# A new memory order for the tiles of a one-core decoder kernel (YOCO trunk, Trainium2)

## The chip, the core and the metric

The kernel runs on one core of a Trainium2 chip. The metric is the device time of one execution in microseconds (us). Three runs of the kernel before gave 1237.50, 1237.68 and 1237.83 us; the median is 1237.68 us.

Five engines take part. PE multiplies matrices (PEld is its loading of weights), DVE does elementwise work and scans, ACT does activations, copies and casts, POOL clears a few tiles and issues some transfers, SP issues most transfers. Each engine works through its own list of instructions in order and waits at an instruction until the semaphores that it names are there.

## The reference, cut to what matters

The input x is 512 tokens by 1024 features. Two layers follow, then a last RMSNorm.

```
x = x + s5_mixer(rms_norm(x))          # layer 0
x = x + conv_ffn(rms_norm(x))
kv = rms_norm(x) @ kv_w                # shared keys and values
x = x + stick_breaking_attention(rms_norm(x), w_q, k, v, w_o)   # layer 1
x = x + conv_ffn(rms_norm(x))
out = rms_norm(x)
```

The mixer projects x (u = h @ w_in), runs a diagonal complex state-space recurrence with 64 states for each group of 16 channels, takes y = C s + D u, then gelu, then a full GLU projection (y @ w_glu, 1024 to 2048). The FFN projects up to 2 x 2816 features, puts a causal convolution of width 3 on the gate half, and projects down to 1024. Attention has 16 heads of 64.

## The kernel before, in words

**Stages.** The work goes through five stages, one after the other: the S5 mixer (lines 241 to 806, the first 225 us), the first FFN, attention, the second FFN, and the final norm inside the last down-projection. x stays on the chip all the time, features on the 128 partitions, 8 tiles of 128 x 512.

**The products.** Nearly all products are float32r products of a split operand: a weight tile is cast into a high part (`split_hi`, L155, on ACT), the rest becomes the low part (`split_lo`, L160, on DVE), and an input is split the same way. `gemm` (L165) then issues three matmuls for each slice of 128 input features: high weight with high input, high weight with low input, low weight with high input. A 128 x 512 output over 8 slices is 24 matmuls. In the profile all of them have line 106. The names of PE's products are: `u` (input projection), `kk`, `v`, `y`, `yt`, `bt` (pieces of the mixer), `gl` (GLU projection), `fg` and `fu` (up-projection, gate and linear half), `fd` (down-projection), `kqb` (keys and queries), `v` (values), `z` (scores) and `ob` (attention output and the output projection).

**Tiles and pools.** A tile of the on-chip memory comes from a pool, by a tag. Each tag of a pool has a fixed number of buffers, and each new tile of the tag takes the next of them in turn; it must wait until the last reader of the tile that was there before is done. Pools lie one above the other in memory in the order in which they are entered. In the kernel before that is, from low to high: `const` (x, parameters), `wp` (raw weights 3 x 4096 bytes, and the high and low weights, 3 x 4096 each), `tp` (split inputs: tag `ta`, 10 tiles of 2048 bytes, and `tb`, 3 of 4096), `sm` (18 small tiles of 16 bytes, for each of which 32 are set aside, and three of 2048), and then the pool of the stage, opened by `Work(name, tag=buffers, ...)` (L60) and closed at its end. Bytes are bytes of each partition here and below. `T` (L83) takes a tile from `tp` or from the stage's pool.

Counted from the tile sizes, the mixer's, the FFN's and the attention's pools begin behind `sm`, so their tiles lie 18 x 32 + 3 x 2048 = 6720 bytes above the end of `tp`, and 6720 is 13 x 512 + 64. In the built program the tiles of `wp` and `tp` begin 160 bytes above a multiple of 512 and those of the stages' pools 224 bytes above one.

**The mixer's loop.** It works in 8 units n (128 channels each), under a hand-written order for PE, DVE and ACT. For unit n, PE issues `kk` and `v_(n + 1)` (L631, 16 products in 32 records, which multiply the two transposed tiles `bts` of unit n + 1 with u; the first 8 read the first `bts`, the other 8 the second), then `y_in(n)`. DVE meanwhile forms `states(n)`: the product `p` of v(n), then `wv`, two additions that combine it (L664 and L665), the scans `rv`, a second `p`, and `xv`, on which PE's `y_state(n)` waits. Beside it DVE works on unit n + 2: `k`, `bn` (from which PE makes the transposes `bt`, copied by ACT into `bts`), `k`, `cm`. Small portions of the projections are put between (`fill`). From 155 us on PE runs the rest of the GLU projection without a break.

**Buffers that the change touches.** In the mixer `bts` has tag `bt` with 2 buffers, `wv` tag `wv` with 1, and `rv`, `xv`, `y8`, `tq` one each. In the FFN the tags `g`, `s` and `u` have 2, 2 and 3 buffers and `a` 24 (the split activations that `fd` reads). In attention `o`, `kv` and `tw` have 2, 2 and 4, and `aw`, `os` and `kq` (split weights of attention, split outputs, split keys and queries) 9, 16 and 8. Attention's own pool `at` (constants, low keys `kl`, values `vv`) is entered behind the stage's pool and lies above it.

Of the kernel before, what the change touches and what calls it, by code (L numbers as in the profile page):

```python
# [7 lines left out]
F32 = mybir.dt.float32  # L8
# [9 lines left out]
P = 128  # L18
S = 512
# [4 lines left out]
EPS = 1e-6  # L24
AW = 22
TP = {"ta": 10}
PRE = (11, 12, 10, 5, 3)
F = ((4, 0, 3, 0), (1, 1, 1, 1), (2, 1, 1, 0), (3, 1, 1, 3), (3, 2, 1, 1), (1, 1, 1, 0), (1, 2, 2, 3), (0, 0, 3, 3))
HALVES = 4
# [18 lines left out]
def trunk(ctx: ExitStack, tc: tile.TileContext, A, out):  # L48
    nc = tc.nc
    V, SC, PE, GP = nc.vector, nc.scalar, nc.tensor, nc.gpsimd  # L50

    const = ctx.enter_context(tc.tile_pool(name="const", bufs=1))
    wp = ctx.enter_context(tc.tile_pool(name="wp", bufs=3))
    tp = ctx.enter_context(tc.tile_pool(name="tp", bufs=1))
    sm = ctx.enter_context(tc.tile_pool(name="sm", bufs=2))
    dr = ctx.enter_context(tc.tile_pool(name="dr", bufs=3, space=DRAM))

    cur = {}

    class Work:  # L60


        def __init__(self, name, **bufs):
            self.name, self.bufs = name, bufs

        def __enter__(self):
            self.pool = tc.tile_pool(name=self.name, bufs=1)
            cur["w"] = (self.pool.__enter__(), self.bufs)

        def __exit__(self, *a):  # L70
            self.pool.__exit__(*a)
# [4 lines left out]
    def banks_by_tag(**bufs):  # L76

        ids = sorted(range(8), key=lambda i: max([n for n, u in enumerate(used) if u == i], default=-1))
        cur["p"] = {}
        for tag, n in bufs.items():  # L80
            cur["p"][tag], ids = ids[:n], ids[n:]

    def T(name, dt=F32, tag=None):  # L83
        if tag in TP:
            return tp.tile([P, S], dt, tag=tag, name=name, bufs=TP[tag])
        pool, bufs = cur["w"]
        return pool.tile([P, S], dt, tag=tag, name=name, bufs=bufs[tag])

# [10 lines left out]
    def B(name, tag="b"):  # L99
        ids = cur["p"][tag]  # L100
        ids.append(ids.pop(0))
        used.append(ids[-1])
        return ps.tile([P, S], F32, tag=f"b{ids[-1]}", name=name, bufs=1)
# [29 lines left out]


    def load_raw(src, cols, name="w", dma=None):
        raw = wp.tile([P, 8 * P], F32, tag="raw", name=name + "r", bufs=3)[:, :cols * P]
        (dma or nc.sync).dma_start(out=raw, in_=src)
        return raw

# [55 lines left out]
    def rstd(b, stag="st"):  # L195
        v = sm.tile([P, 4], F32, name="sv")
        ts(v, b[:, 0:4], 1.0 / 1024.0, EPS, MUL, ADD)
        it = sm.tile([P, 4], I32, name="si")
        ts(it, v.bitcast(I32), 1, op0=ALU.logical_shift_right)
        f = sm.tile([P, 4], F32, name="sf")  # L200
        V.tensor_copy(out=f, in_=it)
        yi = sm.tile([P, 4], I32, name="sy")
        ts(yi, f, -1.0, 1597463007.0, MUL, ADD)
        r = sm.tile([P, 4], F32, name="sr0")
        V.tensor_copy(out=r, in_=yi.bitcast(F32))
        for n in range(3):
            q = sm.tile([P, 4], F32, name="sq2")
            tt(q, r, r, MUL)
            stt(q, q, -0.5, v, MUL, MUL)
            r2 = sm.tile([P, 4], F32, name=f"sr{n + 1}")  # L210
            stt(r2, q, 1.5, r, ADD, MUL)
            r = r2
        dg = N("dg", "sq", 1)
        dg3 = dg.rearrange("p (a c) -> p a c", c=P)
        tt(dg3, bc(ident, 1, [P, 4, P]), bc(r, 2, [P, 4, P]), MUL)
        b2 = B("rbp", stag)
        mm(b2, ones, dg, True, True)
        rb = N("rb", "rb", 1)
        SC.copy(out=rb, in_=b2)
        return rb, r  # L220
# [20 lines left out]
    def s5(st_next):  # L241
        banks_by_tag(st=1, u=2, g=2, kb=1, v=1, y=1)
        with tc.tile_pool(name="s5", bufs=1) as sp, ExitStack() as wctx:
# [19 lines left out]
            u8s, ys = [], []  # L263
# [23 lines left out]
            tags = ("u", "u", "g", "g")  # L287

            def w_load(n, q):
                raw = wp.tile([P, 8 * P], F32, tag="raw", name="wi", bufs=3)  # L290
                for c in ((slice(0, 256), slice(256, 1024)) if n == 0 else (slice(0, 1024),)):
                    q.dma_start(out=raw[:, c], in_=A["w_in"][n][:, c])
                wis.append(raw)
# [41 lines left out]

            def load(k):

                raw = wp.tile([P, 8 * P], F32, tag="raw", name="wvr", bufs=3)
                for i in range(0, HALVES, 2):
                    GP.dma_start(out=raw[:, i * 2 * P:(i + 2) * 2 * P].rearrange("p (h c) -> p h c", h=2),  # L340
                                 in_=A["w_glu"][i // 2, :, :, k * P:(k + 2) * P].rearrange("h p c -> p h c"))
                raws.append(raw)
# [9 lines left out]
            def fill(n):  # L352
                for _ in range(n):
                    next(pe)
# [13 lines left out]
            def evac(now=True):  # L368
                while len(u8s) < (len(bus) if now else evac.ready):
                    u_out(len(u8s))  # L370
                evac.ready = len(bus)

            evac.ready = 0

            fill(PRE[0])
            bst = B("stat", "st")
# [9 lines left out]
            def s32(dt=F32):  # L386
                i = len(small)
                if i % 16 == 0:
                    blocks.append(T("small", tag=("rv", "xv", "y8")[i // 16]))
                small.append(blocks[-1][:, 32 * (i % 16):32 * (i % 16) + 32])  # L390
                return small[i] if dt == F32 else small[i].bitcast(dt)
# [6 lines left out]
            zc, k, r, p = s32(), s32(), s32(), s32()  # L398

            def exp_acc(z):  # L400
                ts(zc, z, -87.0, 88.0, MAX, MIN)
                ts(k, zc, 1.4426950408889634, MAGIC, MUL, ADD)
                ts(k, k, -MAGIC, op0=ADD)
                stt(r, k, -0.693359375, zc, MUL, ADD)
                stt(r, k, 2.12194440054690583e-4, r, MUL, ADD)
                cs = [1.0 / 5040, 1.0 / 720, 1.0 / 120, 1.0 / 24, 1.0 / 6, 0.5, 1.0]
                ts(p, r, cs[0])
                for c in cs[1:]:
                    stt(p, p, c, r, ADD, MUL)
                e = s32(dt=I32)  # L410
                ts(e, k, 127.0, 8388608.0, ADD, MUL)
                o = s32()
                stt(o, p, 1.0, e.bitcast(F32), ADD, MUL)
                return o

            dt = exp_acc(ldt)
# [81 lines left out]
            for g2 in range(2):  # L498
                rows, cols = slice(64 * g2, 64 * g2 + 64), slice(g2, 32, 2)
# [5 lines left out]
            rb, _ = rstd(bst)  # L505
            fill(PRE[1])
            evac()
# [106 lines left out]
            def op_b(n):  # L614

                unit[n] = {}
                k3 = products(b3, pw3, n, 1)
                yield
                bn = wide("bn", 2, "bn")
                sums(bn, k3)  # L620
                unit[n]["b"] = halves(bn)

            def bt_(n, i):
                pb = B("bt", "kb")
                for q in range(4):
                    PE.transpose(v4(pb)[:, q], v4(unit[n]["b"][i])[:, q], ident)
                bt = T("bts", tag="bt")
                SC.copy(out=bt, in_=pb)
                unit[n].setdefault("bt", []).append(bt)
# [98 lines left out]
            def run(gen, n=99):  # L728
                for _ in range(n):
                    if next(gen, True) is True:  # L730
                        return
# [5 lines left out]
            kx_(0)  # L737
            fill(PRE[2])
            bt_(0, 0)
# [5 lines left out]
            run(op_b(1))  # L745
            fill(PRE[3])
            bt_(1, 0)
# [5 lines left out]
            turn_products(1)  # L753
            fill(PRE[4])
            evac()
            decays(0)
            with tc.manual_schedule(engines={E.PE, E.DVE, E.Activation}):
                for n in range(KT):
# [18 lines left out]
                    y8 = y_state(n)  # L777
# [31 lines left out]


    def ffn(layer, prev, st_next):
        with Work(f"ff{layer}", a=24, g=2, acc=2, s=2, u=3, y=8, half=10):
            banks_by_tag(b=7, st=1)
            rb, _ = prev.st.finish()
            ffn_body(layer, prev.xs, rb, st_next)
# [38 lines left out]


    def attention(prev, st_next):
        with Work("att", aw=9, tw=4, os=16, o=2, kq=8, kv=2):
            banks_by_tag(z=6, d0=1, d1=1)
            rb, rtok = prev.st.finish("d0")
            with tc.tile_pool(name="at", bufs=1) as ap:  # L860
                attention_body(ap, prev.xs, rb, rtok, st_next)

    def attention_body(ap, xs, rb, rtok, st_next):
# [16 lines left out]
        class Weight:  # L880
# [2 lines left out]

            def load(self):
                if callable(self.src):
                    self.raw = wp.tile([P, 8 * P], F32, tag="raw", name="awr", bufs=3)
                    self.src(self.raw)
                else:
                    self.raw = load_raw(self.src, self.cols, "aw")
# [127 lines left out]
        kq, vvs, vws = {}, {}, {}  # L1017
# [210 lines left out]
        cur = Head(0)  # L1228
# [7 lines left out]
        with tc.manual_schedule(engines={E.PE, E.DVE, E.Activation}):  # L1236
            pend, late = [4], []
            for i in range(16):
# [79 lines left out]
                cur = nxt  # L1318
# [93 lines left out]

    stages = A.get("stages", 4)
    nx = Next(NFFN0)
    with Work("s5t", ys=16, k=1, bn=1, bt=2, p=1, wv=1, rv=1, xv=1, y8=1, tq=1):
        s5(nx)
    if stages > 1:
        n2 = Next(None)
# [72 lines left out]
```

## Time and profile before

| what | value |
|---|---|
| median of 3 runs | 1237.68 us |
| the profiled execution | 1236.96 us |
| its span, first to last instruction | 1235.2 us |
| mean granted clock of PE | 0.997 |
| PE busy | 1207.6 us, 98% of the span, 6411 records |
| DVE busy | 809.6 us, 66% |
| ACT busy | 539.3 us, 44% |
| DMA | 118.5 MB, 96 GB/s over the span |

The profile is one execution, recorded by the hardware. The profiled execution takes 1.8 us more than its span and 0.7 us less than the median of the runs. A PE record's own duration covers the filling and draining of the array, so the time that a row of matmuls takes is read from start to start: the chain of waits prints it, as the start of a group of instructions, its time on the chain, and the count.

### The profile page before, as it was taken

The numbers are of one execution on the slowest core, as the hardware profiler recorded it, in microseconds if no ns is written. First come the engines' busy times: TensorE is split into PE (matmuls) and PEld (weight loads), VectorE is DVE, ScalarE is ACT, GpSimd is POOL, SyncE is SP. The second block draws the span as 40 slices with busy tenths as digits, with TensorE's granted clock in tenths as the row PEclk, the third lists the DMA queues.
The fourth block names the chain that finished last, engine by engine and source line by source line (L and its number), as shares of the span: only waits on it lengthen the run. The fifth ranks groups of instructions, "written<-read, shape, count | busy, mean of one in ns | idle before, by whom it ended". The sixth has DMA issues, their size and how long they took to land.

```text
span 1235.2 us, 16227 instructions
## 1 busy us (share of the span) xinstructions
PE 1207.6 (98%) x6411; PEld 982.8 (80%) x6411; DVE 809.6 (66%) x1284; ACT 539.3 (44%) x866; POOL 24.2 (2%) x65
## 2 busy tenths in 40 slices
PE   7989999999999999999999999999999999999995
PEld 3457788788888888888889898888888888888884
DVE  7999764665435635557878989878655346536554
ACT  5234453433223323334577878765433233323331
POOL 1011020000000000000000000000000000000000
PEclk9999999999999999999999999999999999999998
DMA  5565443233233233233211211123233232332322
GB/s 199 150 166 140 122 124 98 86 102 98 90 102 99 82 106 101 92 91 100 76 51 53 82 55 48 39 86 103 86 102 97 91 103 86 91 113 88 94 75 69
DMA packets 55068, 118.47 MB, mean 96 GB/s; under 512 B 12912, under 2 KB 28528, under 8 KB 54992
## 3 DMA queue, kind: packets, MB, share of 16 engines
q1 hardware_dynamic: 50880, 105.55, 27.9%
q0 software_dynamic: 3248, 11.54, 3.1%
q8 instruction: 50, 0.82, 0.3%
q10 hardware_dynamic: 864, 0.35, 0.1%
q14 instruction: 26, 0.21, 0.1%
HBM read 109.03 MB, written 8.39 MB: 95 GB/s over the span
## 4 chain that ended last, share of the span: by engine, by line
PE 89%; DVE 8%; ACT 1%; issue 1%; DMA 1%; SPq 0%; DVEq 0%; ACTq 0%
PE fd L106 20%; PE fu L106 19%; PE fg L106 19%; PE kqb L106 7%; PE gl L106 6%; PE z L106 5%; PE ob L106 5%; PE v L106 4%; DVE k L112 2%; DVE p L112 1%; PE u L106 1%; PE y L106 1%; DVE cm L112 1%; DVE u L112 1%; DVE rv L670 1%
## 5 line engine op out<-in xcount | busy, mean ns | idle before, releaser
L106 PE MATMUL fd<-ah,wdh 128*128 128x512 f32 (+1 forms) x359 | 140.5, 391 | 0.0
L106 PE MATMUL fd<-ah,wdl 128*128 128x512 f32 (+1 forms) x359 | 139.2, 388 | 0.0
L106 PE MATMUL fd<-al,wdh 128*128 128x512 f32 (+1 forms) x359 | 137.9, 384 | 0.0
L112 DVE TENSOR_TENSOR x<-x,fd 128x512 f32<-128x512 f32 (+1 forms) x49 | 33.1, 676 | 119.8 <-PE fd L106 119.8
L157 ACT CAST wuh<-wur 128x1024 fp32r<-128x1024 f32 x44 | 46.4, 1054 | 134.4 <-PE fg L106 118.0
L157 ACT CAST wdh<-wdr 128x896 fp32r<-128x896 f32 (+1 forms) x48 | 47.1, 982 | 128.0 <-PE fd L106 98.2
L112 DVE TENSOR_TENSOR g<-fg,rb 128x512 f32<-128x512 f32 x44 | 30.4, 691 | 96.3 <-PE fg L106 93.5
L106 PE MATMUL fu<-xh,wuh 128*128 128x512 f32 x220 | 86.0, 391 | 0.0
L106 PE MATMUL fg<-xh,wgl 128*128 128x512 f32 x220 | 85.8, 390 | 0.0
L106 PE MATMUL fg<-xh,wgh 128*128 128x512 f32 x220 | 85.7, 390 | 0.0
L106 PE MATMUL fg<-xl,wgh 128*128 128x512 f32 x220 | 85.6, 389 | 0.0
L106 PE MATMUL fu<-xh,wul 128*128 128x512 f32 x220 | 85.6, 389 | 0.0
L106 PE MATMUL fu<-xl,wuh 128*128 128x512 f32 x220 | 85.6, 389 | 0.0
L112 DVE TENSOR_TENSOR u<-fu,rb 128x512 f32<-128x512 f32 x44 | 30.4, 691 | 80.5 <-PE fu L106 80.5
L106 PE MATMUL fu<-xhl,wuh 128*128 128x512 f32 x264 | 81.8, 391 | 0.0
L106 PE MATMUL fg<-xhl,wgh 128*128 128x512 f32 x264 | 81.5, 389 | 0.0
L106 PEld LDWEIGHTS fd<-ah,wdl 128*128 128x128 f32 x359 | 67.4, 188 | 15.2
L106 PEld LDWEIGHTS fd<-al,wdh 128*128 128x128 f32 x359 | 67.4, 188 | 14.8 <-issue 0.2
L106 PEld LDWEIGHTS fd<-ah,wdh 128*128 128x128 f32 x359 | 67.5, 188 | 13.2 <-issue 0.2
L157 ACT CAST wgh<-wgr 128x1024 fp32r<-128x1024 f32 x44 | 46.3, 1053 | 71.0 <-PE fd L106 33.0
L106 PE MATMUL u<-xg,wi 128*128 128x512 f32 x128 | 63.5, 628 | 7.5 <-ACT xg L270 7.5
L109 DVE SCALAR_TENSOR_TENSOR acc<-g,cw,acc 128x511 f32<-128x511 f32 x88 | 65.8, 747 | 2.4 <-ACT acc L832 0.9
(247 smaller groups left out, 2799.1 us busy)
## 6 DMA issues: line engine op xcount, KB each, us to landing
wgr<-in_w_up SPq DMA_DIRECT2D x44, 512.0 KB, 3.5
wur<-in_w_up SPq DMA_DIRECT2D x44, 512.0 KB, 3.5
wdr<-in_w_dn SPq DMA_DIRECT2D x32, 448.0 KB, 3.3
wdr<-in_w_dn SPq DMA_DIRECT2D x16, 512.0 KB, 3.5
wvr<-in_w_glu POOLq DMA_DIRECT2D x12, 512.0 KB, 3.8
ks<-kx SPq DMA_DIRECT2D x32, 128.0 KB, 2.5
m<-ks SPq DMA_DIRECT2D x8, 512.0 KB, 4.1
awr<-in_w_k SPq DMA_DIRECT2D x8, 512.0 KB, 3.5
```

The lines of the kernel that those rows point to most:

```text
L106: PE.matmul(o, lhsT=lhsT, rhs=rhs, start=start, stop=stop, skip_group_check=True)
L109: (eng or V).scalar_tensor_tensor(out=o, in0=a, scalar=s, in1=b, op0=op0, op1=op1)
L112: (eng or V).tensor_tensor(out=o, in0=a, in1=b, op=op)
L157: SC.copy(out=hi, in_=raw)
L670: V.tensor_tensor_scan(out=rv[:, c], data0=decay[n], data1=wv[:, c], initial=0.0, op0=MUL, op1=ADD)
```

## The change: what it does

The pools are entered in a new order, low to high: `const`, then `sm`, then a new pool `wr` for the raw weights, then a new pool `lw`, and only then `wp` (now the high and low weights alone), `tp`, and the stages' pools. In attention the pool `at` is entered ahead of the stage's pool, so that constants, low keys and values lie below the other tiles.

The pool `lw` holds tiles that PE mostly doesn't read. It has three tags of 2048-byte tiles: `la` with 2 buffers, `lb` with 2, `lc` with 4. Each `Work` now names which of its tags take their tiles there. In the FFN `g`, `s`, `u` become `la`, `lb`, `lc` (so `u` has 4 buffers where it had 3). In attention `o`, `kv`, `tw` become `la`, `lb`, `lc`, with the counts that they had. In the mixer `rv` becomes `la`; `wv` and `bt` together become `lb`; `tq`, `xv` and `y8` together become `lc`. So the two `bts` of a unit and `wv`, which had three buffers, now take two in turn, and `tq`, `xv`, `y8`, which had three, take four.

No instruction is added or taken away. In the built program the places change as follows (bytes of each partition):

| tiles | before | after |
|---|---|---|
| raw weights | from 34976 | from 41696 |
| high and low weights | 47264 to 71840 | 70368 to 94944 |
| split inputs `xh`, `xl` | 71840 to 92320 | 94944 to 115424 |
| split inputs `xhl` | 92320 to 104608 | 115424 to 127712 |
| GLU inputs `ys` | from 111328 | from 127712 |
| split activations `ah`, `al` | 129760 to 178912 | 131808 to 180960 |
| attention: `kl`, constants, `vv` | 195296 to 221920 | 127712 to 154336 |
| attention: `os` | 162528 to 195296 | 196320 to 229088 |

All tiles behind `sm` begin 224 bytes above a multiple of 512 after the change, the weights and inputs too. So the address of a weight and that of the tile multiplied with it differ, modulo 512, by 64 before and 0 after in `gl`, `fd` and the output projection `ob`; they differ by 0 before and after in `fg`, `fu`, `kqb`, the attention's values `v`, and in the products inside attention.

The diff:

```diff
+LW = {"la": 2, "lb": 2, "lc": 4}
...
     const = ctx.enter_context(tc.tile_pool(name="const", bufs=1))
+
+    sm = ctx.enter_context(tc.tile_pool(name="sm", bufs=2))
+    wr = ctx.enter_context(tc.tile_pool(name="wr", bufs=3))
+    lw = ctx.enter_context(tc.tile_pool(name="lw", bufs=1))
     wp = ctx.enter_context(tc.tile_pool(name="wp", bufs=3))
     tp = ctx.enter_context(tc.tile_pool(name="tp", bufs=1))
-    sm = ctx.enter_context(tc.tile_pool(name="sm", bufs=2))
...
-        def __init__(self, name, **bufs):
-            self.name, self.bufs = name, bufs
+        def __init__(self, name, low, **bufs):
+            self.name, self.low, self.bufs = name, low, bufs
...
-            cur["w"] = (self.pool.__enter__(), self.bufs)
+            cur["w"], cur["low"] = (self.pool.__enter__(), self.bufs), self.low
...
         if tag in TP:
             return tp.tile([P, S], dt, tag=tag, name=name, bufs=TP[tag])
+        if cur["low"].get(tag, tag) in LW:
+            tag = cur["low"].get(tag, tag)
+            return lw.tile([P, S], dt, tag=tag, name=name, bufs=LW[tag])
         pool, bufs = cur["w"]
...
-        raw = wp.tile([P, 8 * P], F32, tag="raw", name=name + "r", bufs=3)[:, :cols * P]
+        raw = wr.tile([P, 8 * P], F32, tag="raw", name=name + "r", bufs=3)[:, :cols * P]
...
-        with Work(f"ff{layer}", a=24, g=2, acc=2, s=2, u=3, y=8, half=10):
+        with Work(f"ff{layer}", {"g": "la", "s": "lb", "u": "lc"}, a=24, acc=2, y=8, half=10):
...
-        with Work("att", aw=9, tw=4, os=16, o=2, kq=8, kv=2):
-            banks_by_tag(z=6, d0=1, d1=1)
-            rb, rtok = prev.st.finish("d0")
-            with tc.tile_pool(name="at", bufs=1) as ap:
+        with tc.tile_pool(name="at", bufs=1) as ap:
+            with Work("att", {"o": "la", "kv": "lb", "tw": "lc"}, aw=9, os=16, kq=8):
+                banks_by_tag(z=6, d0=1, d1=1)
+                rb, rtok = prev.st.finish("d0")
                 attention_body(ap, prev.xs, rb, rtok, st_next)
...
-    with Work("s5t", ys=16, k=1, bn=1, bt=2, p=1, wv=1, rv=1, xv=1, y8=1, tq=1):
+    with Work("s5t", {"rv": "la", "wv": "lb", "bt": "lb", "tq": "lc", "xv": "lc", "y8": "lc"}, ys=16, k=1, bn=1, p=1):
```

The order of the instructions hardly changes, but three places do. The first is on DVE in the mixer's loop, in each unit: `wv` are the two additions of unit n, `p` the product ahead of them, `k` and `bn` the work for unit n + 2, `rv` the scan behind. The names in brackets are the semaphores that an instruction waits for, one for each engine that signals. Before:

```order
L112 TENSOR_TENSOR p<-v,tb 128x1024 [waits PE_49]
L112 TENSOR_TENSOR k<-b_91,pw_255 128x1536 [waits DVE_49]
L112 TENSOR_TENSOR wv<-p 128x256 [waits DVE_49]
L112 TENSOR_TENSOR wv<-p 128x256
L112 TENSOR_TENSOR bn<-k 128x1024 [waits DVE_49,PE_49]
L670 SCALAR_TENSOR_TENSOR rv<-mt,wv 128x256 [waits DVE_49,Pool_49]
```

After (the lines of the changed kernel are 7 higher):

```order
L119 TENSOR_TENSOR p<-v,tb 128x1024 [waits PE_49]
L119 TENSOR_TENSOR k<-b_97,pw_261 128x1536 [waits DVE_49]
L119 TENSOR_TENSOR wv<-p 128x256 [waits DVE_49,PE_49,Activation_49]
L119 TENSOR_TENSOR wv<-p 128x256
L119 TENSOR_TENSOR bn<-k 128x1024 [waits DVE_49]
L677 SCALAR_TENSOR_TENSOR rv<-mt,wv 128x256 [waits DVE_49,Pool_49]
```

The order is the same, but the first `wv` now waits for PE (and for ACT, which wrote the tile that was in the buffer before). With two buffers in turn, `wv` of unit n comes into the buffer of the first `bts` of unit n + 1, whose readers are the first 8 products of `v_(n + 1)`. `bn` no longer names PE, since its wait is covered by that of `wv`.

The second place is on PE in the mixer's last unit: `y` is the product of unit 7 (`m` and `u`, then `cm` and `xv`), `gl` the filling matmuls of the GLU projection around it. Before:

```order
L106 MATMUL gl<-yh,wvl 128x512
L106 MATMUL y<-m_1567,u_1311 64x128 x8
L106 MATMUL y<-cm,xv 64x128 x16
L106 MATMUL gl<-yh,wvh 128x512
L106 MATMUL gl<-yl,wvh 128x512
```

After:

```order
L113 MATMUL gl<-yh,wvh 128x512
L113 MATMUL gl<-yl,wvh 128x512
L113 MATMUL y<-m_1573,u_1317 64x128 x8
L113 MATMUL y<-cm,xv 64x128 x16
L113 MATMUL gl<-yh,wvl 128x512
```

Two `gl` that stood behind `y` before now stand ahead of it.

The third place is on DVE at the start of attention: the casts of the constants `cntri`, `cnones`, `cident` and `cmask`, among the last addition of the first FFN (`x<-x,fd`) and the statistics behind it (`sv`). Before:

```order
L112 TENSOR_TENSOR x<-x,fd 128x512 [waits PE_49]
L112 TENSOR_TENSOR awl<-awr,awh 128x1024 [waits Activation_49]
L112 TENSOR_TENSOR acc<-acc,sq 128x512 [waits Activation_49]
L112 TENSOR_TENSOR xhl<-x,xhl 128x512 [waits DVE_49,Activation_49]
L118 TENSOR_SCALAR sv<-stat 128x4 [waits PE_49]
L871 CAST cntri<-cr 128x128 [waits DMAHW6_49]
```

After:

```order
L119 TENSOR_TENSOR x<-x,fd 128x512 [waits PE_49]
L878 CAST cntri<-cr 128x128
L878 CAST cnones<-cr 128x128 [waits DMAHW0_49]
L119 TENSOR_TENSOR awl<-awr,awh 128x1024 [waits Activation_49]
L119 TENSOR_TENSOR acc<-acc,sq 128x512 [waits Activation_49]
L119 TENSOR_TENSOR xhl<-x,xhl 128x512 [waits DVE_49,Activation_49]
L125 TENSOR_SCALAR sv<-stat 128x4 [waits PE_49]
```

The first two casts moved ahead of `awl`, `acc` and `xhl`; they come directly behind the addition that waits for the last `fd`.

More of the change, by code (lines that the diff above doesn't have):

```diff
@@ L289, in w_load @@
             def w_load(n, q):
-                raw = wp.tile([P, 8 * P], F32, tag="raw", name="wi", bufs=3)
+                raw = wr.tile([P, 8 * P], F32, tag="raw", name="wi", bufs=3)
                 for c in ((slice(0, 256), slice(256, 1024)) if n == 0 else (slice(0, 1024),)):
@@ L336, in load @@
             def load(k):
-                raw = wp.tile([P, 8 * P], F32, tag="raw", name="wvr", bufs=3)
+                raw = wr.tile([P, 8 * P], F32, tag="raw", name="wvr", bufs=3)
                 for i in range(0, HALVES, 2):
@@ L885, in load @@
                 if callable(self.src):
-                    self.raw = wp.tile([P, 8 * P], F32, tag="raw", name="awr", bufs=3)
+                    self.raw = wr.tile([P, 8 * P], F32, tag="raw", name="awr", bufs=3)
                     self.src(self.raw)
```

## The prediction

> **What bounds the kernel now.** First the page of the profile: the busy time of each engine, and the shares of the chain of waits (followed back from the last instruction).
>
> ```profile
> PE 1207.6 (98%) x6411; PEld 982.8 (80%) x6411; DVE 809.6 (66%) x1284; ACT 539.3 (44%) x866; POOL 24.2 (2%) x65
> PE 89%; DVE 8%; ACT 1%; issue 1%; DMA 1%; SPq 0%; DVEq 0%; ACTq 0%
> ```
>
> PE is busy 98% of the span and 89% of the chain is PE's own work, so over most of the kernel time changes only if matmuls follow one another faster or slower. But 8% of the chain is DVE's, and a mean over the span hides where. So second, the busy times by stretch: start and end, length, then PE, PEld, DVE, ACT and POOL with the records in brackets, the granted clock, the DMA share and GB/s.
>
> ```profile
> 50.00:113.00 63.00, 58.28 (x671) 38.05 (x673) 62.59 (x81) 28.93 (x75) 7.62 (x22) 1.00 0.59 163
> 170.00:235.00 65.00, 64.54 (x287) 52.87 (x286) 35.73 (x49) 22.49 (x30) 2.64 (x5) 1.00 0.31 95
> 235.00:588.00 353.00, 352.97 (x1551) 290.62 (x1550) 195.75 (x241) 122.53 (x150) 0.00 (x0) 1.00 0.32 97
> 588.00:858.00 270.00, 269.93 (x1563) 238.19 (x1562) 227.79 (x388) 197.62 (x379) 0.00 (x0) 1.00 0.20 63
> ```
>
> In the mixer's loop, 50 to 113 us, DVE works 62.59 of 63 us: there DVE is the bound. From 170 us on PE has no idle time to speak of, and its granted clock is 1.00. Third, the chain in order of time (start, us on the chain, what) says where the loop hands over:
>
> ```profile
> 98.90 0.06 DVE wv L112
> ...
> 129.99 0.43 DVE xv L112
> ...
> 130.55 1.96 PE y L106 x32
> ...
> 148.42 2.99 PE y L106 x48
> ...
> 154.97 69.57 PE gl L106 x303
> ```
>
> Up to 130 us the chain runs through DVE, then through PE, and from 155 us PE runs 303 GLU matmuls without a break. What the loop loses therefore comes out in full at the end: the GLU matmuls left over are the same, and PE has no idle time behind them in which to catch up.
>
> So there are two things to cost: one new wait on DVE in the loop, and the pace of PE after it.
>
> **The wait that `wv` gets.** `wv` of unit n takes the buffer of the first `bts` of unit n + 1, so it can't start until the first 8 of the 16 products `v` of unit n + 1 are done. Now DVE's `wv` and PE's `v` for these units, a pair of rows for n = 1 to 6 (durations in ns min/median/max of a record, then first and last start in us):
>
> ```profile
> L112 DVE TENSOR_TENSOR wv<-p x2: 414/414/415, 75.3 to 75.7; 128x256 f32<-128x256 f32 x2
> L106 PE MATMUL v<-u,bts x32: 222/222/270, 75.8 to 76.8; 128*64 128x64 f32 x32
> ...
> L112 DVE TENSOR_TENSOR wv<-p x2: 417/418/418, 86.5 to 86.9; 128x256 f32<-128x256 f32 x2
> L106 PE MATMUL v<-u,bts x32: 221/222/270, 87.8 to 88.8; 128*64 128x64 f32 x32
> ...
> L112 DVE TENSOR_TENSOR wv<-p x2: 414/415/416, 98.8 to 99.2; 128x256 f32<-128x256 f32 x2
> L106 PE MATMUL v<-u,bts x32: 222/222/270, 99.3 to 100.2; 128*64 128x64 f32 x32
> ...
> L112 DVE TENSOR_TENSOR wv<-p x2: 421/421/421, 112.1 to 112.4; 128x256 f32<-128x256 f32 x2
> L106 PE MATMUL v<-u,bts x32: 222/222/271, 113.4 to 114.3; 128*64 128x64 f32 x32
> ...
> L112 DVE TENSOR_TENSOR wv<-p x2: 415/415/415, 125.6 to 126.0; 128x256 f32<-128x256 f32 x2
> L106 PE MATMUL v<-u,bts x32: 221/222/271, 126.0 to 126.9; 128*64 128x64 f32 x32
> ...
> L112 DVE TENSOR_TENSOR wv<-p x2: 416/420/424, 135.2 to 135.6; 128x256 f32<-128x256 f32 x2
> L106 PE MATMUL v<-u,bts x32: 222/222/271, 136.9 to 137.9; 128*64 128x64 f32 x32
> ```
>
> In every pair `wv` starts before `v`. A `v` has 32 records whose starts spread over 1.0 us; the 16th starts 0.48 us after the first and takes 0.22 us, so the buffer comes free 0.7 us after the start of `v`. The stalls are 75.8 + 0.7 - 75.3 = 1.2 us for n = 1, and in the same way 2.0, 1.2, 2.0, 1.1 and 2.4 for n = 2 to 6; together 9.9 us. For n = 0 the pair is the other way round:
>
> ```profile
> 60.78 1.15 PE L106 MATMUL v<-u,bts 128*64 128x64 f32 x32
> ...
> 62.20 0.75 DVE L112 TENSOR_TENSOR wv<-p 128x256 f32<-128x256 f32 x2
> ```
>
> 60.78 + 0.7 is before 62.20: no stall. Unit 7 has no `v` of a next unit to wait for.
>
> Do the stalls add up, or does the first one bring DVE behind PE for good? They add up. Behind `wv` on DVE's list stand `bn` of unit n + 2, the scans, the second `p` and `xv`, and PE's `y` of unit n waits for `xv`; PE's `bt`, `yt` and next `v` stand behind that `y`. So a stall moves `xv`, and with it both sides of the next unit's pair, and the gap between them is as before. Nothing covers it: DVE has 0.4 us idle in the 63 us. At unit 6 the wait is PE's to pass on:
>
> ```profile
> 139.18 0.41 DVE L109 SCALAR_TENSOR_TENSOR xv<-p 128x252 f32<-128x252 f32 x1
> ...
> 139.78 1.97 PE L106 MATMUL y<-cm,xv 64*64 64x128 f32 x32
> ...
> PE y L106 <- DMA m<-ks: 0.7, 1, 0.7
> ```
>
> `xv` of unit 6 ends at 139.6 and its `y` starts at 139.8, so 0.2 of the 2.4 us is slack. In unit 7 PE waits 0.7 us for the transfer of `m` ahead of `y`; the two `gl` that now stand ahead of it (about 0.23 us each) fill up to 0.46 of this, I take 0.2. Sum: 9.9 - 0.2 - 0.2 = **+9.5 us**. The ends: 4.8 if a reader sooner than the eighth releases the buffer or PE makes up half, and 12.4 if the wait is for all 16 products (six times 0.5 more).
>
> At the start of attention two casts move ahead of three DVE operations. PE doesn't wait there (269.93 of 270 us busy); I put it at nothing, and its end at 0.9 us, the four casts of 0.22 us.
>
> **PE's pace.** No matmul is added, so this part rests on one comparison in the trace of before. Rows of the same chain:
>
> ```profile
> 309.15 5.44 PE fu L106 x24
> 314.59 43.96 PE fd L106 x192
> 358.55 5.49 PE fg L106 x24
> 364.04 5.44 PE fu L106 x24
> ...
> 434.76 38.47 PE fd L106 x168
> ...
> 842.97 15.17 PE ob L106 x65
> ```
>
> All are 128 x 512 float32r matmuls at a granted clock of 1.00, each with a new weight. `fu` takes 5.44 / 24 = 226.7 ns from start to start, `fd` 43.96 / 192 = 229.0, `gl` 69.57 / 303 = 229.6, and the last output projections 15.17 / 65 = 233.4. The first `fg` behind `fd` takes 0.05 us more than the next ones. What divides them in the code is where the tiles lie: in `fu` and `fg` weight and input begin at the same address modulo 512, in `fd`, `gl` and `ob` 64 bytes apart. The change makes this 0 everywhere. At 226.7 ns the gain would be: in the `fd` of the first chunks 43.96 - 192 x 0.22667 = 0.44 us, twice; of the other chunks 38.47 - 168 x 0.22667 = 0.39, four times; `gl` 69.57 - 303 x 0.22667 = 0.89; `ob`, about 104 matmuls at the rate of the 65, 104 x 6.7 ns = 0.70; `fg` behind `fd` 5 x 0.05 = 0.25. Together **-4.2 us**. The narrow products are at 0 before and after; only the last `fd`, done in halves of 256 columns, may lose: 42 matmuls x 2 ns, under 0.1 us.
>
> That the offset is the cause, and not the region of memory (inputs of `fd`, `gl`, `ob` all lie above 105,000 bytes), I read from narrow matmuls, start, duration and count:
>
> ```profile
> 825.65 0.40 PE L106 MATMUL z<-lh,cnones 128*128 128x256 f32 x2
> ...
> 826.25 0.40 PE L106 MATMUL z<-lh,cntri 128*128 128x512 f32 x1
> ...
> 655.70 5.79 PE v L106 x48
> ...
> 1215.53 0.28 PE L106 MATMUL fd<-ah,wdh 128*128 128x256 f32 x1
> ...
> 1217.89 0.28 PE L106 MATMUL fd<-ah,wdl 128*128 128x256 f32 x1
> ```
>
> Scores `z`, high in memory at offset 0, run 5 matmuls (two rows between are not shown) in 826.25 - 825.65 = 0.60 us, 120 ns each; values `v`, low in memory at offset 0, 5.79 / 48 = 120.6; the last `fd`, high at offset 64, (1217.89 - 1215.53) / 20 = 118.0. High and low agree at the same offset, and the offset that differs gives another pace. Ends of this term: -4.2 us, and the price of the third rival below, +4.9.
>
> The Trainium skill speaks against any gain here: TensorE: Matmul & The Clock Gate, in the part on loading weights, says that PE has two independent read ports, so that loading the next weights takes no read bandwidth from the running matmul; and SBUF — State Buffer, under "two separate sides", that PE never waits on anyone. By these rules addresses would change nothing, and the sum would be +9.5 alone. No run here shows either yet; the 229.0 beside 226.7 for the same instruction is not what they lead one to expect.
>
> **The forecast.** 1236.96 + 9.5 - 4.2 = 1242.3 for an execution like the profiled one, which lies 0.7 us below the median of the runs: **1243.0 us**.
>
> **The rivals.**
> First, the stall comes and the pace stays: `fd`, `gl` and `ob` are slower for a reason of their own (their inputs are freshly written by ACT and DVE, or change with the weight). For it: the only evidence on 512 columns is between stages. Against it: `fg` reads inputs just as still as `fu` does. Time: 1237.7 + 9.5 = 1247.2. This is also the skill's case.
> Second, the stall does not come: PE reaches `v` of the next unit before DVE reaches `wv`. That decides at 1.1 to 2.4 us by which PE would have to be earlier in each unit. It is possible, since PE is idle 4.7 of 63 us there and DVE would be what is late; against it, `v` stands behind the `y` that waits for `xv`, so PE can't run ahead. With the faster pace: 1237.7 - 4.2 = 1233.5, faster than before.
> Third, the region decides: matmuls are slower where the moving tile lies above some 105,000 bytes, and the change moves part of the split inputs there (up to 127,712). Then `fd`, `gl`, `ob` keep their pace and the 2 x 22 x 48 = 2112 up-projections lose up to 229.0 - 226.7 = 2.3 ns each, 4.9 us: 1237.7 + 9.5 + 4.9 = 1252.1. Against it the rows on narrow matmuls.
>
> **How the numbers follow.** Forecast 0.62, first rival 0.22, second 0.10, third 0.06. The predicted time is the first's. Its own range, from the ends of the stall with the whole gain, is 1238.3 to 1245.9. To this comes the first rival's 1247.2; the second and third are left out (0.16). The low end of the stall is unlikely, so the range begins at 1239.0 and ends at 1247.9 (the first rival with a little more stall). About 0.2% (2.5 us) is what a measurement can tell from no change: faster than 1235.2 is the second rival, 0.10; between 1235.2 and 1240.2 lies a half of the stall with the whole gain, 0.06; slower, 0.84.
>
> **What would show it.** In the profile after: `wv` of units 1 to 6 starts 0.6 to 0.9 us behind the first `v` of the next unit, the unbroken GLU run starts near 164.5 us and not 155, DVE shows idle time released by PE `v` in the loop; `fd` takes 43.5 us for 192, `ob` 227 ns, the `fg` behind `fd` 5.44. A GLU run that starts at 155 makes the stall wrong; 43.96 in `fd` makes the pace wrong; an `fu` above 5.44 speaks for the region.

## The result, and the profile after

| | median us | runs, lowest to highest | mean granted clock by run |
|---|---|---|---|
| before | 1237.59 | 6, 1237.01 to 1238.41 | 0.997 in the profiled one |
| after | 1246.82 | 6, 1244.28 to 1247.70 | 0.995 to 0.993 |

The changed kernel takes 1.0071 times as long (95% interval 1.0060 to 1.0082), 9.2 us more. The forecast was 1243.0 us, range 1239.0 to 1247.9. The profiled execution of the changed kernel is the fastest of its six: 1244.28 us, with a span of 1242.5 us and a mean clock of 0.995. The six differ by 3.4 us, and the slower they are, the lower is their mean clock.

First the chain of waits of the changed kernel in order of time, at the places that the prediction showed of before (start, us on the chain, what):

```profile
166.46 68.97 PE gl L113 x302
...
325.51 43.52 PE fd L113 x192
369.03 5.44 PE fg L113 x24
...
445.19 38.08 PE fd L113 x168
...
836.22 30.54 PE ob L113 x137
```

For `ob` the same group of the kernel before reads:

```profile
826.88 31.26 PE ob L106 x137
```

PE's pace came out as forecast: `fd` 43.52 / 192 = 226.7 ns, `fg` behind it 5.44, `ob` 0.72 us less. Only `gl` saved 0.6 us and not 0.9. So the stretches behind the GLU are shorter than before: 1.3 us in each FFN and 1.0 us in attention (starts of `fd`, `kqb` and `fg` rows, after against before). But the unbroken GLU run starts at 166.5 us, not at 155.0 as before and not at 164.5 as forecast. The sum: +11.5 - 0.6 - 1.3 - 1.0 - 1.3 = +7.3 us, the difference of the spans (1242.5 - 1235.2).

The wait that was forecast is there. The list of DVE's waits in the changed kernel between 50 and 165 us, longest sum first (us in all, times, longest), and two of the six `wv` in the timeline (idle time ahead of it, and who ended it, in brackets):

```profile
DVE wv L119 <- PE v L113: 9.9, 6, 2.8
```
```profile
119.02 0.76 DVE L119 TENSOR_TENSOR wv<-p 128x256 f32<-128x256 f32 x2 [1.91 <-PE v L113]
...
135.38 0.76 DVE L119 TENSOR_TENSOR wv<-p 128x256 f32<-128x256 f32 x2 [2.77 <-PE v L113]
```

Six waits, for units 1 to 6, as forecast. The list's sum of 9.9 us equals the 9.9 us of the prediction by chance, though: the fifth wait is 2.77 us where 1.1 were forecast, and the sixth 0.80 where 2.4 were. The sixth is short because a fourth place in DVE's order changed: in unit 6 the low GLU weights (`wvl`) now stand ahead of `wv` and not behind it. Before and after:

```profile
135.24 0.76 DVE L112 TENSOR_TENSOR wv<-p 128x256 f32<-128x256 f32 x2
...
137.10 0.40 DVE L112 TENSOR_TENSOR wvl<-wvr,wvh 128x256 fp32r<-128x256 f32 x1
```
```profile
146.19 0.43 DVE L119 TENSOR_TENSOR wvl<-wvr,wvh 128x256 fp32r<-128x256 f32 x1 [1.23 <-ACT wvh L164]
147.41 0.76 DVE L119 TENSOR_TENSOR wv<-p 128x256 f32<-128x256 f32 x2 [0.80 <-PE v L113]
```

So `wv` of unit 6 starts about 1.23 + 0.43 + 0.80 us behind the `p` ahead of it, the 2.4 us of the forecast, but only 0.8 of them are in the list. From the end of one `xv` to the end of the next, the loop now takes 13.45, 14.42, 13.56, 15.50, 15.01, 10.90 and 5.76 us where it took 12.16, 12.31, 12.29, 13.30, 12.36, 8.86 and 5.83: +1.3, +2.1, +1.3, +2.2, +2.7, +2.0 and -0.1. Forecast were 1.2, 2.0, 1.2, 2.0, 1.1 and 2.2. One of them stands out: the fifth, 2.7 for 1.1. PE's timeline and the busy times by stretch (PE, PEld, DVE, ACT, POOL, granted clock, DMA share, GB/s) of the changed kernel show what happened there:

```profile
125.31 3.50 PE L113 MATMUL y<-cm,xv 64*64 64x128 f32 x32 [2.78 <-DVE xv L119]
```
```profile
120.00:124.00 4.00, 2.53 (x15) 1.63 (x11) 4.00 (x6) 1.33 (x5) 0.45 (x2) 1.00 0.18 39
124.00:128.00 4.00, 2.69 (x26) 2.72 (x28) 4.00 (x8) 0.00 (x0) 0.98 (x4) 0.63 0.70 172
128.00:132.00 4.00, 4.00 (x54) 3.23 (x51) 3.97 (x4) 1.28 (x3) 0.00 (x0) 0.94 0.91 253
```

PE waited 2.78 us for `xv`, and then its `y` took 3.50 us in place of 1.96: the granted clock was 0.63 in this stretch. So the prediction lacks a term. DVE's stall makes PE wait longer, and behind some of these waits PE runs at a lower clock for a few microseconds. The list of PE's waits shows the sum (us in all, times, longest), first of the kernel before, then of the changed one:

```profile
PE y L106 <- DVE xv L112: 6.1, 6, 1.7
```
```profile
PE y L113 <- DVE xv L119: 15.1, 7, 2.9
```

### The profile page after: what moved, and what is told of

It is laid out like the page before. It is cut to its first block, busy times and chain, and to the rows that moved or that the text cites. A ratio compares the mean times of both kernels' runs of the same rounds, so it can differ in the third digit from the quotient of the medians.

```text
span 1242.5 us, 16197 instructions
## 1 busy us (share of the span) xinstructions
PE 1204.3 (97%) x6411; PEld 983.3 (79%) x6411; DVE 809.5 (65%) x1284; ACT 540.2 (43%) x866; POOL 23.9 (2%) x65
## 4 chain that ended last, share of the span: by engine, by line
PE 89%; DVE 8%; ACT 1%; issue 1%; DMA 1%; SPq 0%; DVEq 0%; ACTq 0%
PE fu L113 19%; PE fd L113 19%; PE fg L113 19%; PE gl L113 7%; PE kqb L113 6%; PE ob L113 5%; PE z L113 5%; PE v L113 4%; PE y L113 1%; PE u L113 1%; PE yt L113 1%; DVE p L119 1%; DVE rv L677 1%; DMA x<-in_xT 1%; DVE k L119 1%
## 5 line engine op out<-in xcount | busy, mean ns | idle before, releaser
L119 DVE TENSOR_TENSOR g<-fg,rb 128x512 f32<-128x512 f32 x44 | 30.4, 692 | 96.3 <-PE fg L113 93.6
L113 PEld LDWEIGHTS fd<-ah,wdl 128*128 128x128 f32 x359 | 67.4, 188 | 13.5
```

What stands on the lines that cost most here:

```text
L113: PE.matmul(o, lhsT=lhsT, rhs=rhs, start=start, stop=stop, skip_group_check=True)
L119: (eng or V).tensor_tensor(out=o, in0=a, in1=b, op=op)
```

## The experiments

The theory: the stall costs 9.5 to 10 us; PE's longer gaps let the granted clock drop in some of them, at some 1.5 us each; the addresses save 4.2 us. The rivals: the pace comes from the order or the region in memory, not from the offset; and the excess over the forecast comes from another part of the change, or from DVE.

### The change without the shared buffer

```diff
-    with Work("s5t", {"rv": "la", "wv": "lb", "bt": "lb", "tq": "lc", "xv": "lc", "y8": "lc"}, ys=16, k=1, bn=1, p=1):
+    with Work("s5t", {"rv": "la", "bt": "lb", "tq": "lc", "xv": "lc", "y8": "lc"}, ys=16, k=1, bn=1, p=1, wv=1):
```

> The changed kernel, but wv keeps a buffer of its own in the mixer's pool, so the wait for v is gone and everything else of the change stays. My theory (the stall costs 9.5 to 10 us, makes PE idle longer ahead of y, and the granted clock drops in some of these gaps, which costs up to 3 us more; the new places save 4.2 us): 1237.6 - 4.2 = 1233.4 us, a mean clock of 0.997 and a spread under 1 us. Rival, the excess over the forecast comes from another part of the change (the other shared tags, the start of attention): 1237 us or more.

Measured: 1234.88 us, 0.9973 of before (0.9962 to 0.9984), runs 1232.72 to 1235.55, clock 0.996 to 0.994. No DVE wait of `wv` for `v` is left, and the loop's intervals are those of before within 0.1 us. The excess is gone with the one buffer, so no other part of the change holds more than a small rest of it. The median is 1.5 us over the 1233.4 expected and the spread 2.8 us, more than the 1 us expected.

### The offset alone

One line moved in the kernel before: the pool of the small tiles is entered ahead of `wp`. Nothing that the stages' pools hold changes its place.

```diff
+    sm = ctx.enter_context(tc.tile_pool(name="sm", bufs=2))
     wp = ctx.enter_context(tc.tile_pool(name="wp", bufs=3))
     tp = ctx.enter_context(tc.tile_pool(name="tp", bufs=1))
-    sm = ctx.enter_context(tc.tile_pool(name="sm", bufs=2))
```

> The kernel before, with one line moved: the pool of the small tiles lies below the weights, so weights and inputs go up by 6720 bytes and the stages' tiles stay exactly where they were. All tiles that PE reads then begin at the same address modulo 512. Offset theory: fd 43.52 for 192, ob 227 ns, 1233.4 us. Rival, the order of the pools or the place of raw weights and values makes the pace: 1237.6 us, fd 43.96.

Measured: 1233.44 us, 0.9966 (0.9953 to 0.9978). The chain of this kernel has the fast pace:

```profile
315.40 43.52 PE fd L106 x192
...
435.08 38.08 PE fd L106 x168
...
825.87 30.54 PE ob L106 x137
```

The tiles `ah` and `al` that move through `fd` lie where they lay before, so it isn't their region. And values, raw weights and the other tiles of the change stay in the old order: the order isn't needed.

### The new order with the offset put back

The kernel without the shared buffer, and 64 bytes of padding between the split inputs and the stages' pools:

```diff
+    pd = ctx.enter_context(tc.tile_pool(name="pd", bufs=1))
+    GP.memset(pd.tile([P, 16], F32, name="pad"), 0.0)
```

> The first kernel of this call with a pad of 64 bytes behind the split inputs, so that the whole new order stays but the stages' tiles again lie 64 bytes off modulo 512. Offset theory: fd back at 43.96, gl and ob back, 1237.6 us (4.2 us over the first kernel). Rival, the order makes the pace: 1233.4 us, as the first kernel.

Measured: 1237.98 us, 1.0002 (0.9994 to 1.0011), that is, the time of the kernel before. Its chain:

```profile
315.43 43.96 PE fd L115 x192
...
435.61 38.47 PE fd L115 x168
...
827.94 31.26 PE ob L115 x137
```

To a hundredth of a microsecond these are the old figures, so the faster pace hangs on 64 bytes. The median is 3.1 us over that of the kernel without the padding, where 4.2 were expected; the runs of the two kernels spread over 2.2 and 2.8 us.

### The stall alone

```diff
-                wv = T("wv", tag="wv")
+                wv = T("wv", tag="bt")
...
-    with Work("s5t", ys=16, k=1, bn=1, bt=2, p=1, wv=1, rv=1, xv=1, y8=1, tq=1):
+    with Work("s5t", ys=16, k=1, bn=1, bt=2, p=1, rv=1, xv=1, y8=1, tq=1):
```

> The kernel before, with wv taken from the two buffers of bts in turn and nothing else changed: the stall alone. My theory: 1237.6 + 9.9 = 1247.5 us with no drop of the clock, up to 3.5 us more where it drops, so a median of 1248 to 1251 us, a spread of 2 us or more and a mean clock of 0.993 to 0.996. Rival, the stall costs 9.5 us and the rest came from elsewhere in the change: 1247 us with a spread under 1 us.

Measured: 1251.32 us, 1.0110 (1.0096 to 1.0124), runs 1250.09 to 1253.23, clock 0.994 to 0.991. That is 13.5 us for one buffer, a little more than the 1248 to 1251 us expected. The profiled execution is the slowest of them, and PE's timeline shows three slow `y`, each behind a long wait:

```profile
96.29 3.09 PE L106 MATMUL y<-cm,xv 64*64 64x128 f32 x31 [2.92 <-DVE xv L112]
...
127.03 3.17 PE L106 MATMUL y<-cm,xv 64*64 64x128 f32 x32 [2.78 <-DVE xv L112]
...
142.14 3.68 PE L106 MATMUL y<-cm,xv 64*64 64x128 f32 x32 [2.81 <-DVE xv L112]
```

(The first row holds 31 of the 32 records.) The loop's intervals are 16.1 us longer than before in all. Against the kernel below in whose loop the clock doesn't drop, the three with a slow `y` are longer by 1.6, 1.7 and 2.8 us, together 6.0 us. The other 10.1 us are what the loop of that kernel grew by.

### The changed kernel again

> The changed kernel once more, to stand on the same chip beside the next one, and for a second profile. Expected: 1244.5 to 1249 us; in the profile one to three of the mixer's y take 3.2 to 3.7 us in place of 1.96, each behind a PE gap of over 1.6 us, with a granted clock near 0.6 there.

Measured: 1246.95 us, 1.0069 (1.0056 to 1.0081), runs 1244.15 to 1247.65. The profiled execution (1246.12 us) has two slow `y` where the first one (1244.28 us) had one:

```profile
96.62 2.79 PE L113 MATMUL y<-cm,xv 64*64 64x128 f32 x23 [2.93 <-DVE xv L119]
...
127.18 3.21 PE L113 MATMUL y<-cm,xv 64*64 64x128 f32 x27 [2.78 <-DVE xv L119]
```

(The two rows cover 23 and 27 of the 32 records; in full the two `y` take 3.46 and 3.53 us.) One more drop, 1.8 us more.

### Useless work in PE's gaps

The stall stays as it is, and 42 matmuls whose result nobody reads fill the gaps in which PE waits for `xv`:

```diff
+WARM = (0, 3, 10, 7, 9, 9, 4, 0)
...
                     fill(F[n][0])
+                    if WARM[n]:
+                        dm = B("dm", "kb")
+                        for i in range(WARM[n]):
+                            mm(dm, nid, ys[0][0], i == 0, i == WARM[n] - 1)
                     y8 = y_state(n)
```

> The changed kernel with useless matmuls added on PE, 42 in all, into the gaps in which PE waits for xv (3, 10, 7, 9, 9 and 4 ahead of y of units 1 to 6; they write a bank that nobody reads). The stall of DVE stays. Theory, the excess over the forecast is the granted clock that drops when PE idles: the clock stays at 0.997, no y takes over 2.1 us, and the time falls to about 1243.3 us with a spread under 1.5 us although PE does 9.5 us more work. Rival, the excess is DVE's (longer stalls in some executions): 1247 us or more, spread as before.

Measured: 1241.81 us, 1.0033 of before (1.0021 to 1.0046), runs 1241.52 to 1242.68, 5.1 us under the 1246.95 of the changed kernel measured beside it. One of PE's `y`, the stretches of the loop and DVE's wait in this kernel:

```profile
125.53 1.97 PE L114 MATMUL y<-cm,xv 64*64 64x128 f32 x32 [0.74 <-DVE xv L120]
```
```profile
50.00:113.00 63.00, 58.02 (x636) 38.09 (x634) 58.12 (x75) 26.20 (x71) 7.51 (x23) 1.00 0.56 149
113.00:170.00 57.00, 54.82 (x642) 43.63 (x641) 39.84 (x59) 24.97 (x60) 4.05 (x14) 1.00 0.40 112
```
```profile
DVE wv L120 <- PE v L114: 8.4, 6, 2.1
```

No `y` is slow, the clock in the loop is 1.00, and the spread is 1.2 us. The rival with DVE's own longer stalls is out, since only PE's gaps were filled. DVE's wait fell with them: it was 9.9 and 11.4 us in the two profiles of the changed kernel, because a slow `y` delays the `v` behind it, for which the next `wv` waits. Without slow `y` the six waits are 1.2, 2.1, 1.2, 1.9, 1.2 and 0.8 us, and the loop is 10.1 us longer than before. The profiled execution takes 1242.37 us, 5.4 us more than the profiled one of before; 9.5 - 4.2 = 5.3 was the sum in the prediction. It isn't free of a drop altogether: from 11.9 to 15.3 us, ahead of the loop, its clock is 0.50, and its first `xv` is 0.4 us later than in the profile of before. The median is 1.5 us under the 1243.3 that I expected, and of that I have no account; one part may be the start, where PE waits for `xg`, the input of its first products, 6.9 to 8.5 us in most of the profiles.

### The same in the version without the stall

Small fillings (2, 3, 2 and 6 matmuls ahead of `y` of units 2 to 5) in the kernel with `wv` in its own buffer.

> The new order of the pools with wv in a buffer of its own, and useless matmuls in the remaining gaps of PE (2, 3, 2 and 6 ahead of y of units 2 to 5). If gaps of 1.7 us already let the clock drop at times, the spread of 1232.7 to 1235.6 without them narrows and the median falls to about 1233 us. Rival, the clock drops in other places (the start, the end): 1234.9 us, spread as before.

Measured: 1233.45 us, 0.9964 (0.9950 to 0.9977), runs 1232.93 to 1234.33, beside 0.9973 (0.9962 to 0.9984) without the filling. The intervals overlap: that this filling gains anything is not settled. That a drop can come behind a gap of 1.7 us is shown by the profiled execution of the kernel with the small tiles below:

```profile
130.53 3.55 PE L106 MATMUL y<-cm,xv 64*64 64x128 f32 x32 [1.70 <-DVE xv L112]
```

### Other offsets

Paddings between the split inputs and the stages' pools give other differences. 128, 192 and 256 bytes are the kernel before with 64, 128 and 192 bytes of padding; 32 is the kernel with the small tiles below and 32 bytes of padding.

> The kernel before with a pad of 64 bytes behind the small tiles, so that the stages' tiles lie 128 bytes from the weights modulo 512 in place of 64. If the pace repeats every 128 bytes or less: fd 43.52 for 192 and 1233.4 us. If only a full 512 (or 256) counts: fd 43.9 or more and 1237.6 us or slower.

> The kernel before with the small tiles below the weights and a pad of 32 bytes behind the split inputs: 32 bytes of difference modulo 512. So far 0 gave 43.52 us for the fd of 192, 64 gave 43.96, 128 gave 44.79. If the pace falls off steadily with the difference: 43.7. If any difference costs the same 0.44: 43.96. If 32 bytes are below the step that counts: 43.52.

> The kernel before with the stages' tiles 192 bytes from the weights modulo 512. If the cost grows with the difference: fd of 192 above 44.79 us. If it repeats at 256: as at 64, 43.96.

> The kernel before with the stages' tiles 256 bytes from the weights modulo 512. If the pace repeats every 256 bytes: fd of 192 in 43.52 us. If it is largest half-way: above 44.79.

Measured, the `fd` of 192 in the four chains, at 128, 32, 192 and 256 bytes:

```profile
315.48 44.79 PE fd L108 x192
```
```profile
316.69 44.80 PE fd L108 x192
```
```profile
316.69 44.80 PE fd L108 x192
```
```profile
314.14 43.52 PE fd L108 x192
```

For `ob`, at 128 and 32 bytes:

```profile
829.98 31.26 PE ob L108 x137
```
```profile
831.73 31.37 PE ob L108 x137
```

| difference modulo 512, bytes | 0 | 32 | 64 | 128 | 192 | 256 |
|---|---|---|---|---|---|---|
| `fd`, ns from start to start | 226.7 | 233.3 | 229.0 | 233.3 | 233.3 | 226.7 |
| time, us | 1233.4 | 1244.0 | 1237.6 | 1242.9 | 1243.8 | 1232.9 |

At 128 bytes the ratio is 1.0042 (1.0028 to 1.0055); at 32, 192 and 256 the time is one execution each, beside one of before at 1237.52. At 256 bytes the fast pace is back, and on the way there it does not fall off steadily: in `fd`, 64 is the mildest of the wrong differences that were tried. At 192, which is 64 on the other side of 256, `fd` takes 44.80 and not the 43.96 expected for that case. The three guesses for 32 bytes (43.52, 43.7, 43.96) were all wrong. The kernel before stood at a half-good place by chance, and only in part: its `ob` takes 31.26 us at 64 as at 128, and in the rows of the prediction its last 65 matmuls take 233.4 ns each at a difference of 64, where `fd` takes 229.0. So the difference separates the fast pace from the slow ones; which slow pace comes at 64 isn't told by it alone, and that stays open.

## Why the prediction was right, and what it lacked

**The wait: right in mechanism and size.** Six stalls, none for units 0 and 7. The fair comparison is the kernel with filled gaps, in whose loop the clock doesn't drop: with the 2.4 us by which `wv` of unit 6 comes late, its stalls are 10.0 us for 9.9 forecast. They add up, as argued: the intervals of its loop grew by 1.3, 2.2, 1.3, 2.2, 1.1 and 2.0 us. In its profiled execution the stall and the pace together gave 5.4 us, for 5.3 forecast. The 9.9 us in the list of the changed kernel are the same figure by luck, as said above.

**The pace: right.** Forecast -4.2; in the profiles the parts are -0.6 (`gl`), -1.3, -1.0 and -1.3, together -4.2. `gl` was put 0.3 us too high, attention 0.3 too low. The offset as the cause was shown from three sides: alone, taken back, and swept. The prediction took it for the whole cause and passed over its own 233.4 ns for `ob` beside 229.0 for `fd` at the same 64 bytes. The move of the first casts at the start of attention cost nothing that shows.

**The sum: a term was missing.** "Sum: 9.9 - 0.2 - 0.2 = +9.5 us" prices DVE's stall and takes PE to lose only that time. I read PE's granted clock of 1.00 in the trace of before and carried it over to a loop in which PE waits 15.1 us for `xv` and not 6.1. In the changed kernel the clock drops behind one gap or more; a drop lengthens the loop by 1.5 to 1.6 us there (15.01 for 13.46 us in the first profile, 15.05 for 13.56 and for 13.46 in the second, against the intervals with filled gaps). With two of them the forecast of 1243.0 becomes 1246.1, and the median is 1246.8. Counted from the 1241.8 of the kernel with filled gaps, the 5.1 us would be three drops rather than two. Filling the gaps took the drops of the loop away and 5.1 us with them, which shows the cause; how many drops a usual run has is not shown, since only runs with one and two of them were profiled.

**The range: met by luck in part.** The median of 1246.8 lies in the stated range (1239.0 to 1247.9), but that range was stretched upward for the first rival, which fell. The range that the prediction gave to its own mechanism, 1238.3 to 1245.9, misses the median by 0.9 us.

**The first rival: its time was nearly met, for a reason that wasn't there.** "The stall comes and the pace stays" gave 1247.2 us, 0.4 us from the median. But its row is refuted: `fd` takes 43.52 and not 43.96. A gain of 4.2 us was there and a loss of about the same size lay over it. The time alone would have confirmed the wrong story.

**The second and third rivals fell.** DVE waited in six units, and `fu` takes 5.44 us with its inputs up to 127,712 bytes.

The rules that the prediction set against the gain, in the Trainium skill, SBUF — State Buffer, section "SBUF: two separate sides" (PE never waits on anyone), and TensorE: Matmul & The Clock Gate, on the two read ports, would have given 1247.2 us. The measurement decides against what I drew from them: the same matmuls at the same granted clock take 226.7, 229.0 or 233.3 ns, and only the difference of two addresses was changed.

## What to carry to other kernels

When two tags come to share buffers, look in the trace for who reads the old tile last and when, on both engines: a pair of rows for each turn of the loop gives the stall, and if both sides hang on the same earlier event, the stalls add up. When a wait moves to PE, price the gap and the clock behind it too; an engine that idles in a loop bounded by another may cost more than its idle time, and even useless matmuls can then pay. And before a layout is judged by its order, work out the addresses modulo 256 of what PE loads and what moves through it: padding of a few bytes was worth 4 to 6 us here, in either direction, and the whole useful part of this change is one line (1233.4 us).

## What the hardware showed that I had not expected

The pace of 128 x 512 float32r matmuls with a new weight each time depends on the difference between the addresses of weight and moving tile: in `fd` 226.7 ns at 0 and 256 bytes, 229.0 at 64, 233.3 at 32, 128 and 192; in the last `ob` 233.4 at 64. Other differences were not tried; that everything repeats every 256 bytes is read from this one pair.

The granted clock dropped behind PE gaps of 1.70, 2.78, 2.81, 2.92 and 2.93 us, but not behind each of them: in the first profile of the changed kernel a gap of 2.92 us and one of 2.81 us passed without a drop. The Trainium skill, TensorE: Matmul & The Clock Gate, section "HAM oscillation — how this bites in real kernels", speaks of gaps of over about 3.4 us; here shorter ones were enough.

The traces show in part what set these gaps apart. In each of them the clock changes only at points that lie a multiple of 3.41 us from one another: in the second profile of the changed kernel it is 0.50 from 96.3 to 99.7 us and again from 127.0 to 130.4, nine such steps later. The slow `y` that lost 2.8 us, in the kernel with the stall alone, had two steps at 0.50 behind one another, from 141.3 to 148.1 us, the second although PE was busy for 2.52 us of the first. Here are steps of the first profile of the changed kernel with the step behind each:

```profile
94.35:97.76 3.41, 1.51 (x28) 1.54 (x30) 3.38 (x7) 0.00 (x0) 1.41 (x2) 1.00 0.92 223
97.77:101.17 3.40, 3.40 (x52) 2.40 (x48) 3.37 (x4) 1.57 (x3) 0.23 (x2) 1.00 0.67 232
...
121.66:125.07 3.41, 0.87 (x4) 0.38 (x2) 3.41 (x6) 0.71 (x2) 0.65 (x2) 1.00 0.52 113
125.08:128.48 3.40, 3.17 (x30) 3.20 (x32) 3.40 (x6) 0.00 (x0) 0.78 (x3) 0.50 0.67 163
```

The gap of 2.92 us (93.3 to 96.3) was shared between two steps, and PE was busy for 1.51 us of the emptier one; the gap of 2.78 us (122.5 to 125.3) lay almost whole in one step, with 0.87 us busy, and the clock was halved for the next. In the loops of all profiles five steps have PE busy for 0.87 us or less, and a step at half clock follows each of them. Where PE was busy for 1.49 to 1.70 us the clock was halved behind two steps (1.49 and 1.70 us) and not behind others (1.49, 1.51, 1.70). What decides between those stays open, and no run moved the steps against the loop.
